# Layer 0's scan output and z gate kept as features by tokens: two heads on the two halves of the array, both directions' states in one product, the RMS norm applied to the projection's result

## The chip, the cores and the metric

The kernel runs on one core of one Trainium2 chip. The metric is the device time of one execution, in microseconds (us). Lower is better. The engines of the core have a queue each and work through it in order: TensorE (PE, with its weight loads PEld), VectorE (DVE), ScalarE (ACT), GpSimd (POOL), and SyncE (SP), which issues the transfers.

## What is computed

Two layers of a diffusion trunk for 1024 latent tokens and 128 context tokens, width 1024, all in float32. Only layer 0's second branch matters here, a bidirectional Mamba-2 scan with 16 heads of 64 features, 2 groups and a state of 64, in chunks of 128 tokens. Cut down:

```python
decay = exp(where(causal, cum[l] - cum[s], -inf))          # per head, direction, chunk of 128 tokens
scores = einsum("bclhn,bcshn->bclsh", C, B) * decay
y_diag = einsum("bclsh,bcshp->bclhp", scores, x * dt)      # inside the chunk
y_off = einsum("bclhn,bchpn,bclh->bclhp", C, h_in, exp(cum))   # from the state that enters the chunk
y = y_fwd + flip(y_bwd) + d_skip[:, None] * x
s_out = rms_norm(y * silu(z), gnorm_w)                     # over the 1024 features of a token
out = concat([a_out, s_out]) @ w_out                       # a_out: the attention branch, 512 features
```

There are nine chunks: eight of latent tokens (numbers 0 to 7) and one of context tokens (number 8, `NLT`), which has no entering state.

## The kernel before

Products with weights are float32 made of two rounded parts (`split` makes a high part on ACT and a low part on DVE), three matmuls each (`mm3`, L256 to L258). Float32 matmuls that are not split appear in the trace as two instructions each.

The program is written as one stream of calls. A scheduler sets each engine's queue from it; `weave` mixes two generators call by call. Tiles are taken by tag with a number of buffers, and whoever takes the tag's next buffer waits for its last reader. The stages, in order of time:

1. Norm, modulation, keys and values of layer 0.
2. `queries` (18 calls) woven with `zproj`. `zproj` makes the gate z in four slabs of 256 columns. For each slab and each of nine token tiles, `tok_proj` runs 24 matmuls with tokens as the stationary operand and 256 moving columns; ACT takes a tanh, DVE finishes the silu (without its factor), and a transfer stores 128 tokens by 256 features in `z_d`.
3. `convs` beside `attention0`: the depthwise convolution makes x, B and C as features by tokens. x is transposed on TensorE and stored as tokens by features in `xs_d`; B and C go to `bc_d`, the states that enter the chunks to `H_d`.
4. `gates0` (attention's gate) woven with `first_outputs`, which runs `scan_out` for the context chunk and for latent chunk 0.
5. The loop that the change is about most: for each chunk c from 1 to 7 `scan_out(c)` stands beside `project_out` of the chunk before it. After the loop follow the last `project_out` and layer 1's latents.
6. Layer 1, which the change does not touch.

`scan_out(c)` loads the chunk's B and C (`BC`), x (`xs`), z (`zs`) and the entering states of both directions (`Hc`: 64 rows for each direction). `Gp` is the product of C and B for the two groups. A "head group" below is four heads, four to a chunk. For each, `cu` (two buffers) is loaded with the cumulated decays of both directions, broadcast to all partitions (L1000). POOL masks each direction (L1003), ACT takes eight exponentials (L1005), DVE adds the two directions (L1007) and multiplies by `G` (L1008), and four matmuls with these 128x128 scores as the stationary operand and 64 columns of x give `yacc` (L1011). The entering states come in through `off`: for each half of the heads and each direction one matmul with 64 rows and 512 columns (L992), scaled by exp(cum) on DVE (L994) and added to y on POOL (L995). At the end DVE adds `yacc` and multiplies by z (L1012, L1013), ACT squares and sums (L1015), POOL makes the reciprocal root (L391, L392), DVE scales y (L1017), TensorE transposes it (L1022) and `split` writes `sT`.

`project_out` accumulates 12 blocks of 128 features (4 of attention, 8 of the scan) in one bank for each half of the columns, and `residual` multiplies by the gate on DVE (L1060) and adds on POOL (L1061). Then come the norm for layer 1 (L1094, L1096) and `norm_T` (L1049, L1052, L1053), which transposes and stores to `h1_d`.

Of the kernel before, what the change touches and what calls it, by code (L numbers as in the profile page):

```python
# [220 lines left out]
def hybrid_trunk(ctx: ExitStack, tc: tile.TileContext, I, O, dbg=None, stage=99):  # L221
# [60 lines left out]
    z_d = scratch("z_d", [T, D])  # L282
# [105 lines left out]
    def rstd_of(p, ssq, n, width):  # L388

        r = p.tile([128, width], F32, tag="rstd", name="rstd", bufs=4)  # L390
        pool.tensor_scalar(r, ssq, 1.0 / n, EPS, ALU.mult, ALU.add)  # L391
        pool.tensor_tensor(r, r, minus_half, ALU.pow)  # L392
        return r
# [81 lines left out]

    lp = Space(mem, right=True)
    nb = lp.tile([128, 2, W16], F32, name="nb", at="F")
    ex = lp.tile([128, 2, W16], F32, name="ex", at="F")
    dskip = lp.tile([128, 16], F32, name="dskip", at="F")
    wdt = lp.tile([128, 2, W16], F32, name="wdt", at="F")  # L480
    decL = lp.tile([128, NLT, 16], F32, name="decL", at="F")
    dma.dma_start(dskip, bcast_rows(I["ab_d_skip"][0], 128))

    def coefficients(p):
# [34 lines left out]
        for d in range(2):  # L519
# [4 lines left out]
            act.activation(ex[:, d], pt[:, 0:W16], AF.Exp)  # L524
# [17 lines left out]
    with Space(mem) as p:  # L542
# [159 lines left out]

    def fm_proj(w, b, hT, c):

        acc = psum("mm", "acc")
        ws = slice(b * 128, (b + 1) * 128)
        for k in range(KT):
            mm3(acc[:, 0:CH], w[0][:, k, ws], w[1][:, k, ws], hT[c][0][:, k], hT[c][1][:, k], k == 0, k == KT - 1)
        return acc[:, 0:CH]
# [137 lines left out]
    def convs(p):  # L847
# [18 lines left out]
        for n, sb in enumerate(order):  # L866
            for b in range(2):
# [19 lines left out]
                if fb < 9:  # L887
# [74 lines left out]
    heads = lambda v: v.rearrange("p (h d) -> p h d", d=64)  # L962
    sTs = {}

    def scan_out(p, sp, c):
        tok = slice(c * 128, (c + 1) * 128)
# [11 lines left out]
        zs = p.tile([128, D], F32, tag="zs", name="zs", bufs=2)  # L978
        dma.dma_start(zs, z_d[tok])
# [4 lines left out]
        y = p.tile([128, D], F32, tag="y", name="y", bufs=2)  # L984
        pool.tensor_tensor(heads(y), heads(xs), dskip.unsqueeze(2).broadcast_to([128, 16, 64]), ALU.mult)
        for g in range(2):
            cs = slice(g * 512, (g + 1) * 512)
            if c < NLT:
                for d in range(2):
                    off = psum("pre", "off")  # L990
                    ds = slice(d * 64, (d + 1) * 64)
                    pe.matmul(off, BC[ds, 1, g], H[ds, cs], start=True, stop=True)  # L992
                    t = p.tile([128, 512], F32, tag="rt", name="off", bufs=2)
                    dve.tensor_tensor(heads(t), heads(off), ex[:, d, c * 16 + g * 8:c * 16 + g * 8 + 8].unsqueeze(2).broadcast_to([128, 8, 64]), ALU.mult)  # L994
                    pool.tensor_tensor(y[:, cs], y[:, cs], t, ALU.add)  # L995
            acc = psum("o" if c < NLT else "pre", "yacc")
            for u in range(2):
                h0 = c * 16 + g * 8 + u * 4
                cu = p.tile([128, 4, 2, 128], F32, tag="cu", name="cu", bufs=2)
                dma.dma_start(cu, bcast_rows(cum_d[h0:h0 + 4], 128))  # L1000
                for d in range(2):
                    s = 1 - 2 * d
                    pool.affine_select(cu[:, :, d], cu[:, :, d], [[0, 4], [s, 128]], ALU.is_ge, NEG, base=0, channel_multiplier=-s)  # L1003
                    for j in range(4):
                        act.activation(cu[:, j, d], cu[:, j, d], AF.Exp, bias=nb[:, d, h0 + j:h0 + j + 1])  # L1005
                m = cu[:, :, 0]
                dve.tensor_tensor(m, m, cu[:, :, 1], ALU.add)  # L1007
                dve.tensor_tensor(m, m, G[:, g].unsqueeze(1).broadcast_to([128, 4, 128]), ALU.mult)  # L1008
                for j in range(4):
                    hc = (u * 4 + j) * 64  # L1010
                    pe.matmul(acc[:, hc:hc + 64], m[:, j], xs[:, g * 512 + hc:g * 512 + hc + 64], start=(u == 0 and j == 0), stop=(u == 1 and j == 3))  # L1011
            dve.tensor_tensor(y[:, cs], acc, y[:, cs], ALU.add)  # L1012
            dve.tensor_tensor(y[:, cs], y[:, cs], zs[:, cs], ALU.mult)  # L1013
        ssq = p.tile([128, 1], F32, tag="ssq", name="ssq", bufs=4)
        act.activation(zs, y, AF.Square, accum_out=ssq)  # L1015
# [680 lines left out]
```

## Time and profile before

| | before |
|---|---|
| median of three runs | 1849.1 us (1843.53 to 1849.83) |
| the profiled execution | 1849.66 us, its span from first to last instruction 1847.8 us |
| mean granted TensorE clock | 0.958 |
| TensorE busy | 1713.8 us, 93% of the span |
| VectorE, ScalarE, GpSimd busy | 1045.4 us, 817.2 us, 744.2 us |
| the stage of queries and z | about 90 to 300 us of the span |
| convolutions and layer 0's attention | about 300 to 630 us |
| attention's gates and the first two scans | about 630 to 768 us |
| five even rounds of the loop of scan and projection | about 768 to 922 us |

Matmuls are pipelined and their ends are modelled, so a busy TensorE is not a full one: what a matmul costs is read from one start to the next. The rows of a stage tell more than the page's shares, since the stages have different limits.

### The profile page before, as it was taken

The page shows a single profiled execution, that of the slowest core. Times are in us where ns is not written, and L with a number is a line of the kernel's source. Part 1 is how long each engine was busy: PE and PEld are TensorE (multiplying, and loading weights), DVE is VectorE, ACT ScalarE, POOL GpSimd, SP SyncE. Part 2 cuts the span into 40 slices and gives each one's busy share as a digit, 9 for nine tenths or more (in the row PEclk, how much of TensorE's full clock was granted, in tenths as well). Part 3 has the DMA queues.
Part 4 walks back from the last instruction along what each step waited for, and adds up shares of the span by engine and source line. Part 5 has one row for each costly group of instructions (what it writes and reads, how often), then busy time and mean ns, then how long its engine had stood idle before and what let it go on. Part 6 is the DMA issues. An engine that isn't in the chain of part 4 may idle for free.

```text
span 1847.8 us, 27078 instructions
## 1 busy us (share of the span) xinstructions
PE 1713.8 (93%) x9031; PEld 1315.1 (71%) x9031; DVE 1045.4 (57%) x1989; ACT 817.2 (44%) x1873; POOL 744.2 (40%) x741
## 2 busy tenths in 40 slices
PE   6899999999998878998899999999999998998898
PEld 3799999877775766666688898655665665654486
DVE  4665545655546467777665434655665664564243
ACT  4532323665655354444444322444545544545321
POOL 3510000133343345665623010466666665565432
PEclk9999999999999888999999999899999998999899
DMA  7423423434435697565463532020120121104342
GB/s 260 125 81 93 121 62 111 131 101 132 115 105 146 195 284 240 166 208 159 167 180 85 165 110 79 11 61 23 52 71 23 45 75 28 37 29 122 109 154 91
DMA packets 210655, 210.26 MB, mean 114 GB/s; under 512 B 36162, under 2 KB 175504, under 8 KB 210516
## 3 DMA queue, kind: packets, MB, share of 16 engines
q1 hardware_dynamic: 210372, 208.40, 37.8%
q8 instruction: 72, 1.18, 0.3%
q14 instruction: 67, 0.55, 0.1%
q0 software_dynamic: 144, 0.13, 0.0%
HBM read 151.94 MB, written 51.72 MB: 110 GB/s over the span
## 4 chain that ended last, share of the span: by engine, by line
PE 65%; DMA 11%; DVE 8%; POOL 4%; ACT 3%; issue 3%; SPq 2%; POOLq 0%; DVEq 0%; ACTq 0%
PE acc L256 12%; PE acc L258 12%; PE acc L257 12%; PE acco L1469 6%; PE sc L1448 3%; PE pp L1427 3%; PE sc L1450 3%; PE sc L1449 3%; DMA arenaG<-cum_d 2%; DVE arenaR L250 2%; DMA arenaF<-rd_d 2%; DMA rd_d<-arenaF 2%; PE st L808 1%; DVE arenaF L209 1%; POOL arenaG L1003 1%
## 5 line engine op out<-in xcount | busy, mean ns | idle before, releaser
L256 PE MATMUL acc<-arenaR 128*128 128x384 f32 (+4 forms) x1248 | 426.7, 343 | 20.0 <-ACT arenaR L249 8.0
L1484 POOL TENSOR_TENSOR arenaG<-arenaG 128x512 f32<-128x512 f32 x256 | 332.6, 1318 | 233.8 <-ACT arenaG L1455 201.1
L257 PE MATMUL acc<-arenaR 128*128 128x384 f32 (+3 forms) x1176 | 398.2, 339 | 0.1
L258 PE MATMUL acc<-arenaR 128*128 128x384 f32 (+4 forms) x1152 | 385.9, 336 | 0.2
L256 PEld LDWEIGHTS acc<-arenaR 128*128 128x128 f32 x1248 | 240.0, 193 | 61.7 <-issue 16.0
L1455 ACT ACTIVATE arenaG<-sc 128x512 f32<-128x512 f32 (+1 forms) x304 | 174.7, 580 | 224.2 <-PE sc L1450 206.7
L209 DVE TENSOR_REDUCE arenaF<-pp 128x1 f32<-128x384 f32 (+1 forms) x400 | 198.8, 539 | 102.2 <-PE pp L1427 100.2
L257 PEld LDWEIGHTS acc<-arenaR 128*128 128x128 f32 x1176 | 226.4, 193 | 15.7 <-issue 3.6
L258 PEld LDWEIGHTS acc<-arenaR 128*128 128x128 f32 x1152 | 221.6, 192 | 16.5 <-DVE arenaR L250 2.3
L250 DVE TENSOR_TENSOR arenaR<-arenaF,arenaR 128x512 fp32r<-128x512 f32 (+2 forms) x144 | 133.2, 938 | 73.3 <-ACT arenaR L249 68.5
L249 ACT CAST arenaR<-arenaF 128x512 fp32r<-128x512 f32 (+3 forms) x160 | 101.0, 649 | 138.9 <-issue 22.6
L1469 PE MATMUL acco<-arenaG 128*64 128x512 f32 (+1 forms) x608 | 152.0, 612 | 0.0
L1005 ACT ACTIVATE arenaG<-arenaG,arenaF 128x128 f32<-128x128 f32 x288 | 88.4, 389 | 113.0 <-POOL arenaG L1003 112.7
L1427 PE MATMUL pp<-arenaR 96*128 96x384 f32 (+1 forms) x300 | 97.6, 387 | 12.8 <-DVE arenaF L209 12.5
L749 POOL TENSOR_TENSOR arenaG<-arenaF,arenaG 128x512 fp32r<-128x512 f32 x28 | 47.8, 1708 | 150.8 <-PE acco L753 87.0
L1448 PE MATMUL sc<-arenaR 96*128 96x512 f32 (+1 forms) x228 | 94.9, 416 | 5.6 <-ACT arenaG L1455 5.4
L1427 PEld LDWEIGHTS pp<-arenaR 96*128 96x128 f32 x300 | 58.6, 203 | 57.3 <-DVE arenaF L209 28.4
L1450 PE MATMUL sc<-arenaR 97*128 97x512 f32 (+1 forms) x228 | 90.6, 400 | 1.0 <-DMA arenaR<-arenaF 1.0
L258 PE MATMUL acc<-arenaR,arenaS 128*128 128x512 f32 (+1 forms) x240 | 90.6, 382 | 0.0
L1449 PE MATMUL sc<-arenaR 96*128 96x512 f32 (+1 forms) x228 | 89.9, 394 | 0.0
L1469 PEld LDWEIGHTS acco<-arenaG 128*64 128x64 f32 x608 | 37.3, 141 | 71.4 <-issue 68.3
L1003 POOL TENSOR_SCALAR_AFFINE_SELECT arenaG<-arenaG 128x512 f32<-128x512 f32 x72 | 60.2, 859 | 63.3 <-DMA arenaG<-cum_d 56.4
(328 smaller groups left out, 3331.9 us busy)
## 6 DMA issues: line engine op xcount, KB each, us to landing
arenaF<-in_ada_w_dram SPq DMA_DIRECT2D x96, 256.0 KB
arenaG<-cum_d SPq DMA_DIRECT2D x36, 512.0 KB
arenaF<-in_ab_w_in_dram SPq DMA_DIRECT2D x51, 256.0 KB
z_d<-arenaF SPq DMA_DIRECT2D x36, 128.0 KB
xs_d<-arenaF SPq DMA_DIRECT2D x8, 576.0 KB
arenaF<-xs_d SPq DMA_DIRECT2D x9, 512.0 KB
arenaF<-z_d SPq DMA_DIRECT2D x9, 512.0 KB
x_d<-arenaG SPq DMA_DIRECT2D x9, 512.0 KB
```

The source lines that it names most:

```text
L209: f()
L250: lo_eng.tensor_tensor(lo, src, hi.bitcast(F32), ALU.subtract)
L256: pe.matmul(out, ah, bh, start=first, stop=False)
L257: pe.matmul(out, ah, bl, start=False, stop=False)
L258: pe.matmul(out, al, bh, start=False, stop=last)
L1427: pe.matmul(pp[:, 0:w], AQ[s][0:96, t * 128:(t + 1) * 128], AK[s][0:96, k0:k0 + w], start=True, stop=True)
L1448: pe.matmul(sc[:, 0:n], AK[s][0:96, ks], BQ[s][:, qs], start=True, stop=False)
L1449: pe.matmul(sc[:, 0:n], BK[s][:, ks], AQ[s][0:96, qs], start=False, stop=False)
L1450: pe.matmul(sc[:, 0:n], AK[s][:, ks], AQ[s][:, qs], start=False, stop=True)
L1455: act.activation(pf, sc[:, 0:n], AF.Exp, scale=SCALE_M)
L1469: put = lambda: pe.matmul(acc[0][a * 64:(a + 1) * 64], V[:, a], pfs[a], start=(i < 2 and k < 2), stop=(last and k >= len(todo) - 2))
L1484: pool.tensor_tensor(totals[a], first[a] if i == 1 else totals[a], pfs[a], ALU.add)
```

## The change

- `zproj` uses `fm_proj`: the slab's weights are the stationary operand and 384 tokens move, so z comes out as features by tokens. 24 calls take the place of 36, and `z_d` is eight blocks of 128 features by all tokens.
- `convs` stores x as features by tokens too (`xT_d`), and `scan_out` loads it into `y` and multiplies it by `d_skip` there.
- `yacc` is now features by tokens: 64 features of a head are the stationary operand (64 columns) and the 128x128 scores move. Heads alternate between partitions 0 to 63 and 64 to 127 of the accumulator, that is between the halves of the array's columns.
- The states come in by the same accumulation: `Cx` is exp(cum) of both directions (two ACT instructions of 64 partitions, L1008) times C (one DVE instruction, L1009); its 128 rows are the two directions' 64 states, so one matmul for each head takes in both. L992, L994, L995 and the table `ex` are gone.
- y is not scaled and not transposed. `split` takes it as it is. Its squares are summed over feature blocks on DVE (L1031) and over partitions by a matmul with ones (L1033); ACT copies the sum (L1035).
- `project_out` accumulates attention's part and the scan's part in two banks; ACT copies the first (L1105), DVE multiplies the second by the token's norm factor and adds (L1106), POOL multiplies by the gate (L1107) and adds (L1108).

```diff
         def zproj(zp, w):
             for q in range(4):
-                for t in range(NT):
-                    acc = tok_proj(t, w, 256)
-                    th = zp.tile([128, 256], F32, tag="zth", name="zth", bufs=3)
-                    act.activation(th, acc, AF.Tanh)
-                    dve.scalar_tensor_tensor(th, th, 1.0, acc, ALU.add, ALU.mult)
-                    dma.dma_start(z_d[t * 128:(t + 1) * 128, q * 256:(q + 1) * 256], th)
-                    if t == 6 and q < 3:
-                        wn = zw(q + 1)
-                    yield
+                for b in range(2):
+                    for c in range(NCH):
+                        acc = fm_proj(w, b, hT, c)
+                        th = zp.tile([128, CH], F32, tag="zth", name="zth", bufs=3)
+                        act.activation(th, acc, AF.Tanh)
+                        dve.scalar_tensor_tensor(th, th, 1.0, acc, ALU.add, ALU.mult)
+                        dma.dma_start(z_d[q * 2 + b, :, c * CH:(c + 1) * CH], th)
+                        if b and c == 1 and q < 3:
+                            wn = zw(q + 1)
+                        yield
...
-            weave(queries(qp, wq), 18, zproj(qp, wz), 36)
+            weave(queries(qp, wq), 18, zproj(qp, wz), 24)
...
                     if fb < 8:
+                        dma.dma_start(xT_d[fb][:, 0:NL], th[:, 0:NL])
+                        dma.dma_start(xT_d[fb][:, NL:T], th[:, NL + 2:W])
...
-        for g in range(2):
-            cs = slice(g * 512, (g + 1) * 512)
+        for u in range(4):
+            g, h0 = u // 2, c * 16 + u * 4
+            if u % 2 == 0:
+                acc = psum("o" if c < NLT else "pre", "yacc")
+            cu = p.tile([128, 4, 2, 128], F32, tag="cu", name="cu", bufs=2)
+            dma.dma_start(cu, bcast_rows(cum_d[h0:h0 + 4], 128))
             if c < NLT:
+                Cx = p.tile([128, 4, 128], F32, tag="Cx", name="Cx", bufs=2)
                 for d in range(2):
-                    off = psum("pre", "off")
-                    ds = slice(d * 64, (d + 1) * 64)
-                    pe.matmul(off, BC[ds, 1, g], H[ds, cs], start=True, stop=True)
-                    t = p.tile([128, 512], F32, tag="rt", name="off", bufs=2)
-                    dve.tensor_tensor(heads(t), heads(off), ex[:, d, c * 16 + g * 8:c * 16 + g * 8 + 8].unsqueeze(2).broadcast_to([128, 8, 64]), ALU.mult)
-                    pool.tensor_tensor(y[:, cs], y[:, cs], t, ALU.add)
+                    r = slice(d * 64, (d + 1) * 64)
+                    act.activation(Cx[r], cu[r, :, d], AF.Exp)
+                dve.tensor_tensor(Cx, Cx, BC[:, 1, g].unsqueeze(1).broadcast_to([128, 4, 128]), ALU.mult)
...
+            todo = [(xs, m, j) for j in range(4)] + ([(H, Cx, j) for j in range(4)] if c < NLT else [])
+            for n, (left, right, j) in enumerate(todo):
+                a, b = j % 2, u % 2 * 2 + j // 2
+                in_order(n, acc[a * 64:(a + 1) * 64, b * 128:(b + 1) * 128], left[:, (u * 4 + j) * 64:(u * 4 + j + 1) * 64], right[:, j],
+                         start=(u % 2 == 0 and n < 2), stop=(u % 2 == 1 and n >= len(todo) - 2))
...
-        dve.tensor_scalar(y, y, r, None, ALU.mult)
-        sT = sp.tile([128, 2, KT, 128], F32R, tag="sT", name="sT", bufs=2)
-        for q in range(2):
-            pt = psum("tr", "pt")
-            for j in range(4):
-                pe.transpose(pt[:, j * 128:(j + 1) * 128], y[:, (q * 4 + j) * 128:(q * 4 + j + 1) * 128], ident)
-            split(sT[:, 0, q * 4:q * 4 + 4], sT[:, 1, q * 4:q * 4 + 4], pt.rearrange("p (k n) -> p k n", k=4))
+        sT = sp.tile([128, 2, KT, 128], F32R, tag="sT", name="sT", bufs=2)
+        split(sT[:, 0], sT[:, 1], y)
+        act.activation(zs, y, AF.Square)
+        sq = p.tile([128, 128], F32, tag="sq", name="sq", bufs=1, at="G")
+        dve.tensor_reduce(sq, zs.rearrange("p k n -> p n k"), AX.X, ALU.add)
+        pt = psum("tr", "pt")
+        pe.matmul(pt[:, 0:1], sq, one, start=True, stop=True)
...
-            acc = psum("mm", "acc")
-            for k in range(12):
-                h, l = (at[:, 0, k], at[:, 1, k]) if k < 4 else (sT[:, 0, k - 4], sT[:, 1, k - 4])
-                mm3(acc, h, l, *wos[k, q], k == 0, k == 11)
-            residual(p, q, acc, x, gate)
+            plain, scaled = psum("pre", "acca"), psum("mm", "accs")
+            for k in range(4):
+                mm3(plain, at[:, 0, k], at[:, 1, k], *wos[k, q], k == 0, k == 3)
+            for k in range(8):
+                mm3(scaled, sT[:, 0, k], sT[:, 1, k], *wos[k + 4, q], k == 0, k == 7)
+            tmp = p.tile([128, 512], F32, tag="rt", name="rt", bufs=2)
+            act.copy(tmp, plain)
+            dve.scalar_tensor_tensor(tmp, scaled, r, tmp, ALU.mult, ALU.add)
+            pool.tensor_tensor(tmp, tmp, gate[:, cs], ALU.mult)
+            pool.tensor_tensor(x[:, cs], x[:, cs], tmp, ALU.add)
```

How the queues stand in the loop, at three places. In these rows a float32 matmul is one row entry, not two. First TensorE at the end of a scan. Before (L256 to L258 are `project_out`'s products, L1049 layer 1's transposes):

```order
L992 MATMUL off<-arenaG,arenaF 128x512
L973 MATMUL Gp<-arenaF 128x128 x2
L1011 MATMUL yacc<-arenaF,arenaG 128x64 x4
L1022 MATMUL pt<-ident,arenaF 128x128 x8
L992 MATMUL off<-arenaG,arenaF 128x512 x2
L256 MATMUL acc<-arenaR,arenaS 128x512
```

TensorE with the change, at a head group between the products of a projection:

```order
L256 MATMUL accs<-arenaR,arenaS 128x512
L257 MATMUL accs<-arenaR,arenaS 128x512
L258 MATMUL accs<-arenaR,arenaS 128x512
L984 MATMUL Gp<-arenaF 128x128 x2
L971 MATMUL yacc<-arenaG,arenaF 64x128 x4
L971 MATMUL yacc<-arenaG 64x128 x4
```

The transposes of y and the four products of the states are gone, and each head group has eight matmuls of 128 moving columns (L971 is the helper `in_order`); in some rounds two groups stand one behind the other.

VectorE at the end of a scan, before (L1096 and L250 into arenaR belong to `project_out`):

```order
L1017 TENSOR_SCALAR arenaF<-arenaF 128x1024
L994 TENSOR_TENSOR arenaG<-off,arenaF 128x512
L1007 TENSOR_TENSOR arenaG<-arenaG 128x4x128
L1096 TENSOR_SCALAR arenaG<-arenaG,arenaF 128x1024
L250 TENSOR_TENSOR arenaR<-arenaG,arenaR 128x512
L1008 TENSOR_TENSOR arenaG<-arenaG,arenaF 128x4x128
```

VectorE behind the end of a scan with the change (L1016 and L1017 are now the two steps of the scores, L1116 the former L1096):

```order
L250 TENSOR_TENSOR arenaS<-arenaF,arenaS 128x1024
L1031 TENSOR_REDUCE arenaG<-arenaG 128x128
L1116 TENSOR_SCALAR arenaG<-arenaG,arenaF 128x1024
L1009 TENSOR_TENSOR arenaG<-arenaG,arenaF 128x512
L250 TENSOR_TENSOR arenaR<-arenaG,arenaR 128x512
L1016 TENSOR_TENSOR arenaG<-arenaG 128x4x128
L1017 TENSOR_TENSOR arenaG<-arenaG,arenaF 128x4x128
```

The two steps of the scores stand together here, and the norm's steps stand ahead of the next group's scores instead of between its two steps.

ScalarE over one round before, beginning with three head groups' exponentials:

```order
L1005 ACTIVATE arenaG<-arenaG,arenaF 128x128 x24
L1015 ACTIVATE arenaF<-arenaF 128x1024
L1094 ACTIVATE arenaG,arenaF<-arenaG 128x1024
L1005 ACTIVATE arenaG<-arenaG,arenaF 128x128 x8
L249 CAST arenaR<-arenaG 128x512
L975 COPY arenaF<-Gp 128x256
L249 CAST arenaS<-pt 128x512 x2
```

ScalarE with the change, from the end of one scan into the next:

```order
L1014 ACTIVATE arenaG<-arenaG,arenaF 128x128 x8
L1114 ACTIVATE arenaG,arenaF<-arenaG 128x1024
L249 CAST arenaS<-arenaF 128x1024
L1029 ACTIVATE arenaG<-arenaF 128x1024
L1008 ACTIVATE arenaG<-arenaG 64x512 x2
L1008 ACTIVATE arenaF<-arenaG 64x512 x2
L1014 ACTIVATE arenaG<-arenaG,arenaF 128x128 x16
L1035 COPY arenaF<-pt 128x1
L1105 COPY arenaF<-acca 128x512
```

Two exponentials for `Cx` (L1008) now stand ahead of each head group's eight (L1014), and L1012, POOL's mask, can overwrite a direction of `cu` only behind the exponential that reads it.

More of the change, by code (lines that the diff above doesn't have):

```diff
@@ L388, in rstd_of @@
     def rstd_of(p, ssq, n, width):
[L390 removed]
+        r = p.tile([128, width], F32, tag="rstd", name="rstd", bufs=5)
         pool.tensor_scalar(r, ssq, 1.0 / n, EPS, ALU.mult, ALU.add)
@@ L474, in tok_proj, with fm_proj @@
         return acc[:, 0:n]
+    def fm_proj(w, b, hT, c):
+        acc = psum("mm", "acc")
+        ws = slice(b * 128, (b + 1) * 128)
+        for k in range(KT):
+            mm3(acc[:, 0:CH], w[0][:, k, ws], w[1][:, k, ws], hT[c][0][:, k], hT[c][1][:, k], k == 0, k == KT - 1)
+        return acc[:, 0:CH]
     lp = Space(mem, right=True)
     nb = lp.tile([128, 2, W16], F32, name="nb", at="F")
-    ex = lp.tile([128, 2, W16], F32, name="ex", at="F")
-    dskip = lp.tile([128, 16], F32, name="dskip", at="F")
+    dskip = lp.tile([128, KT], F32, name="dskip", at="F")
+    one = lp.tile([128, 1], F32, name="one", at="F")
+    pool.memset(one, 1.0)
     wdt = lp.tile([128, 2, W16], F32, name="wdt", at="F")
     decL = lp.tile([128, NLT, 16], F32, name="decL", at="F")
-    dma.dma_start(dskip, bcast_rows(I["ab_d_skip"][0], 128))
+    for a in range(2):
+        dma.dma_start(dskip[a * 64:(a + 1) * 64], bcast_rows(I["ab_d_skip"][0].rearrange("(b a) -> a b", a=2)[a], 64))
     def coefficients(p):
@@ L700, in hybrid_trunk @@
         return
-    def fm_proj(w, b, hT, c):
-        acc = psum("mm", "acc")
[L706 to L709, printed above, removed]
     def silu_of(sp, acc):
@@ L960, in gates0, with in_order @@
             yield
-    heads = lambda v: v.rearrange("p (h d) -> p h d", d=64)
-    sTs = {}
+    sTs, rs = {}, {}
+    def in_order(n, *a, **k):
+        m = pe.matmul(*a, **k)
+        if n:
+            tc.keep_in_program_order(m)
     def scan_out(p, sp, c):
@@ L995, in scan_out @@
[L995 to L1003, printed above, removed]
-                    for j in range(4):
[L1005 to L1008, printed above, removed]
-                for j in range(4):
-                    hc = (u * 4 + j) * 64
-                    pe.matmul(acc[:, hc:hc + 64], m[:, j], xs[:, g * 512 + hc:g * 512 + hc + 64], start=(u == 0 and j == 0), stop=(u == 1 and j == 3))
@@ new lines, in scan_out @@
+                    act.activation(Cx[r], cu[r, :, d], AF.Exp)
+                dve.tensor_tensor(Cx, Cx, BC[:, 1, g].unsqueeze(1).broadcast_to([128, 4, 128]), ALU.mult)
+            for d in range(2):
+                s = 1 - 2 * d
+                pool.affine_select(cu[:, :, d], cu[:, :, d], [[0, 4], [s, 128]], ALU.is_ge, NEG, base=0, channel_multiplier=-s)
+                for j in range(4):
+                    act.activation(cu[:, j, d], cu[:, j, d], AF.Exp, bias=nb[:, d, h0 + j:h0 + j + 1])
@@ L1039, in hybrid_trunk @@
     if stage <= 4:
-        dbg("S", a_d, H_d, cum_d, ex, nb)
+        dbg("S", a_d, H_d, cum_d, nb)
         return
@@ L1049, in norm_T @@
                 pe.transpose(pt[:, j * 128:(j + 1) * 128], xh[:, (q * 4 + j) * 128:(q * 4 + j + 1) * 128], ident)
-            full = p.tile([128, 4, 128], F32, tag="nf", name="nf", bufs=1)
+            full = p.tile([128, 4, 128], F32, tag="rt", name="nf", bufs=2)
             bc = lambda v: v[:, l, q * 4:q * 4 + 4, cond].unsqueeze(2).broadcast_to([128, 4, 128])
```

32 lines of the change are left out of this document (19 added, 13 removed).

## The prediction

> **What bounds the kernel now.** I read the page first, then the stages' busy times, then the chain of work and the waits of the loop, then TensorE's starts in order of time. The page:
>
> ```profile
> PE 1713.8 (93%) x9031; PEld 1315.1 (71%) x9031; DVE 1045.4 (57%) x1989; ACT 817.2 (44%) x1873; POOL 744.2 (40%) x741
> ```
>
> TensorE is the busiest by far, so the question for each stage is whether it is full there. Busy time of the engines in three stages (columns: from and to, length, busy PE, PEld, DVE, ACT, POOL with instructions, granted clock, DMA share, GB/s):
>
> ```profile
> 90.00:300.00 210.00, 208.83 (x1691) 206.52 (x1690) 116.36 (x365) 62.98 (x181) 16.47 (x27) 1.00 0.32 96
> 630.00:768.00 138.00, 120.31 (x553) 96.15 (x553) 92.31 (x129) 63.84 (x163) 68.90 (x68) 0.86 0.76 234
> 768.00:922.00 154.00, 136.41 (x654) 103.79 (x652) 111.57 (x135) 67.22 (x198) 95.81 (x96) 0.94 0.54 174
> ```
>
> In the stage of queries and z TensorE never stops (208.8 of 210). In the first two scans (630 to 768) it is idle 18 us, with the DMA engines at 0.76. The loop (768 to 922) is five rounds. Its chain of work, over one round and a bit:
>
> ```profile
> 772.46 1.10 PE yacc L1011 x8
> ...
> 804.13 1.10 PE yacc L1011 x8
> ...
> 813.68 0.85 PE yacc L1011 x8
> ...
> 814.65 3.66 DMA arenaG<-cum_d
> ...
> 824.72 1.23 POOL arenaG L995
> ...
> 829.11 1.68 DVE arenaG L1096
> 830.78 2.31 DVE arenaR L250
> ...
> 834.18 1.10 PE yacc L1011 x8
> ```
>
> The same place comes back at 772.46, 804.13 and 834.18: a round is (834.18 - 772.46) / 2 = 30.9 us. From 804.13 to 814.5 the chain is TensorE's; then a head group frees its `cu` buffer, the next load takes 3.66, and mask, exponentials, the states' sum on POOL and the norm's steps on VectorE follow until TensorE gets its scores at 834.18. So a round hangs on both TensorE's order and the way of one head group. Who waits there (us in total over five rounds, times, longest):
>
> ```profile
> ACT arenaG L1005 <- POOL arenaG L1003: 76.1, 16, 8.7
> PE yacc L1011 <- DVE arenaG L1008: 11.6, 5, 2.9
> DVE arenaG L1017 <- POOL arenaF L392: 8.8, 3, 2.9
> ...
> PE pt L1022 <- DVE arenaG L1017: 3.8, 3, 1.3
> PE pt L1022 <- DVE arenaF L1017: 2.2, 2, 1.2
> ```
>
> TensorE waits once a round for scores (11.6 / 5 = 2.3 us) and once for the scaled y (6.0 / 5 = 1.2), because VectorE stands 2.9 us before L1017 until POOL has the norm's factor.
>
> **The change part by part.** *z.* The starts of z's matmuls now, 256 columns (first two rows, three apart), and of 384 columns as `fm_proj` runs them in another stage (last two, nine apart):
>
> ```profile
> 270.78 0.28 PE L256 MATMUL acc<-arenaS,arenaR 128*128 128x256 f32 x1
> 271.14 0.28 PE L256 MATMUL acc<-arenaS,arenaR 128*128 128x256 f32 x1
> ...
> 1099.79 0.33 PE L258 MATMUL acc<-arenaR 128*128 128x384 f32 x1
> 1101.35 0.33 PE L258 MATMUL acc<-arenaR 128*128 128x384 f32 x1
> ```
>
> That is 0.12 and 0.173 us each. Before, 36 x 24 = 864 at 0.12 = 103.7; with the change 24 x 24 = 576 at 0.173 = 99.7. TensorE is full there, so 4 us less, of which I take 3.6, since the clock and the mix vary. The cover that shrinks is the next slab's: it is asked for two z calls ahead of its use now (2 x 24 x 0.12 = 5.8 us, with a query between), then one (4.2 us). If its arrival fell short by the difference at all three slabs, 4.8 us would be lost; queries' matmuls stand between and hide it, so I take nothing. ACT and VectorE have fewer and larger pieces and stay far from full.
>
> *TensorE in the loop.* One round's pieces (starts, so that modelled ends don't count):
>
> ```profile
> 816.95 1.00 PE L1011 MATMUL yacc<-arenaF,arenaG 128*128 128x64 f32 x8
> 817.88 1.12 PE L992 MATMUL off<-arenaG,arenaF 64*128 64x512 f32 x2
> 818.93 0.50 PE L256 MATMUL acc<-arenaR 128*128 128x512 f32 x1
> ...
> 827.96 1.58 PE L1022 MATMUL pt<-ident,arenaF 128*128 128x128 f32 x8 [1.22 <-DVE arenaF L1017]
> 829.47 2.08 PE L992 MATMUL off<-arenaG,arenaF 64*128 64x512 f32 x4
> 831.48 0.65 PE L256 MATMUL acc<-arenaR,arenaS 128*128 128x512 f32 x1
> ...
> 1235.23 0.40 PE L1449 MATMUL sc<-arenaS,arenaR 96*128 96x512 f32 x1
> 1235.56 0.44 PE L1469 MATMUL acco<-arenaG 128*64 128x128 f32 x4
> 1235.93 0.27 PE L1412 MATMUL pt<-ident,arenaF 128*4 128x128 f32 x1
> ```
>
> Scores: four groups at 817.88 - 816.95 = 0.93, 3.7 us. States: eight instructions, two at 1.05 twice and four at 2.01, 4.1 us. Transposes of y: 1.51. Together 9.3 us a round. The new form is in the trace already: layer 1's L1469, 64 stationary columns, 128 moving, heads alternating between halves, four instructions in 1235.93 - 1235.56 = 0.37 with the way in and out. A head group has 16: 1.48, four groups 5.9, and the two instructions of L1033 as two of L1011, 0.23: 6.1 us. TensorE saves 3.2 us a round.
>
> The price's ends come from the chain of work, one form that stays on one half and L1469 with 512 columns:
>
> ```profile
> 475.16 1.24 PE st L808 x10
> ...
> 1173.56 1.87 PE acco L1469 x8
> ```
>
> Without any overlap of halves 64 x 0.124 + 0.23 = 8.2 (saves 1.1); with a quarter of the 512-column price, 64 x 1.87 / 8 / 4 + 0.23 = 4.0 (saves 5.3). I take L1469 with 128 columns, the same shape.
>
> Here a rule speaks against the change. Between L1449 and the four L1469 stand 0.33 us, where 0.23 is usual, so going into the halves costs about 0.1. The Trainium skill, TensorEngine Tiling (Array Packing), Key Properties, says that "Changing tiling mode (not just tile) drains the TensorE". Were a drain a whole matmul's 0.40 (the row of L1449) on each way in and out, eight a round, it would take 3.2 us, all of the saving; the trace's 0.37 for four with both ways agrees with a short drain only.
>
> *The other engines in the loop.* Rows of the groups over the five rounds, and below them the nearest rows of the whole trace:
>
> ```profile
> L1008 DVE TENSOR_TENSOR arenaG<-arenaG,arenaF 128x512 f32<-128x512 f32 x20 | 20.4, 1020 | 0.5
> L994 DVE TENSOR_TENSOR arenaG<-off,arenaF 128x512 f32<-128x512 f32 x20 | 13.7, 682 | 6.0 <-POOL arenaG L1061 6.0
> ...
> L250 DVE TENSOR_TENSOR arenaS<-pt,arenaS 128x512 fp32r<-128x512 f32 x10 | 6.4, 675 | 0.0
> ```
> ```profile
> L250 DVE TENSOR_TENSOR arenaR<-arenaF,arenaR 128x1024 fp32r<-128x1024 f32 x15 | 25.4, 1693 | 19.1 <-ACT arenaR L249 19.0
> L824 ACT COPY arenaS<-st 64x512 f32<-64x512 f32 x16 | 9.2, 577 | 10.4 <-PE st L808 10.3
> L209 DVE TENSOR_REDUCE arenaF<-pp 128x1 f32<-128x384 f32 x384 | 195.2, 549 | 101.1 <-PE pp L1427 99.3
> ```
>
> VectorE has 111.6 / 5 = 22.3 us a round. It loses L994 (4 x 0.68 = 2.7), two lows of `sT` (1.35) and L1017 with its wait; it gains L1009 four times (as L1008, 4.1), the low of `sT` in one (1.7) and L1031 (1024 elements against 384: 1.5): about 25 us, still under the round. ScalarE has 13.4 and gains eight `Cx` exponentials at 0.58 (4.6) and two copies (1.2): about 19. POOL has 19.2, loses four L995 (1.2 each) and gains two products by the gate (as L995 too): about 17. The transfers grow by 512 KB a round; a round at 174 GB/s is 5.4 MB, so by a tenth, at a share of 0.54.
>
> *Waits.* The 1.2 us before the transposes goes with them. The wait for scores stays and its way gets longer: two exponentials stand ahead of the masks, 2 x 0.58 = 1.2 us, and VectorE's added work, (25 - 22.3) / 4 = 0.6 for a group. What is late next is that group's L1017. So a round gains 3.2 + 1.2 - 1.2 - 0.6 = 2.6 us. Seven scans (chunks 1 to 7) stand beside projections: 18 us.
>
> *The first two scans.* TensorE has 18 us to spare there, so its saving counts nothing; 1 MB more for x (4.5 us at 234 GB/s if transfers set the end, nothing if they don't) is hidden by the same spare time. I take 0, with -4 to +4.5 as ends. The 4.7 MB of x stored in the convolutions' stage, 16 more issues on SP's queue, lie behind 330 us of TensorE's work: 0.
>
> Sum: 3.6 + 18.2 = 21.8 us off the profiled execution's 1849.66, 1827.9. The median of the runs is 0.6 lower, 1849.1, so I say 1828.
>
> **The rivals.** *The loop doesn't move, only z does.* What TensorE gives up turns into waits, as the chain leaves TensorE for 20 of 31 us already. For it: 76.1 us of waits of ACT behind POOL's masks. Against: TensorE's own order is the chain from 804.13 to 814.5, and two waits a round fall away. 1849.1 - 3.6 = 1845. A drain at 0.40 each way ends here too.
>
> *Slower: head groups that stand in pairs.* The queue with the change has two groups' exponentials behind each other in some rounds. With both `cu` buffers freed together, ScalarE does 2 x (1.2 + 2.45) in a row (2.45 is one group's eight), and TensorE has nothing else ready: the second group comes 1.2 + 1.2 later than now, 2.4 us a round with no TensorE saving seen, 7 x 2.4 - 3.6 = +13: 1862. It decides where load, ScalarE's 7.3 and VectorE's two steps for the second group (as L1008, 1.0 each: 3.7 + 7.3 + 2.0 = 13.0) are longer than what TensorE has to do between two pairs, half a round without waits and savings: (30.9 - 3.5 - 3.2) / 2 = 12.1. That is close, but only some rounds have pairs. The row of the eight:
>
> ```profile
> 819.11 2.45 ACT L1005 ACTIVATE arenaG<-arenaG,arenaF 128x128 f32<-128x128 f32 x8 [6.41 <-POOL arenaG L1003]
> ```
>
> *Much faster.* The norm's factor no longer stops VectorE, its scores come in time, and a round falls to VectorE's 25 us: 7 x 5.9 + 3.6 = 45, 1804. Against: no engine in the loop runs at more than nine tenths now.
>
> **How the numbers follow.** Forecast 0.62 (own range 1815 to 1840: 1.0 to 4.4 us a round, the first scans' ends), only z 0.18, slower 0.12, much faster 0.08. From 1806 to 1850 leaves out most of the slow case and the lower half of the much faster one, under 2 in 10. A measurement tells about 0.5%, 9 us: faster than 1840 has 0.69 (0.62 x 0.98 and 0.08), within 0.19, slower 0.12.
>
> **What would show it.** Right: rounds of about 28 us; L971 groups of 16 in about 1.5 us from start to start; the stage of queries and z about 3.6 us shorter; no engine waiting for L392 at the end of a scan. Wrong: 16 instructions taking 2 us; rounds at 31 with TensorE's waits for L1017 grown by what it saved; TensorE idle before a slab's first matmul in z; transfers of x and z late in the first two scans.

## The result: slower by 1.15%, and the profile after

The changed kernel takes 1871.7 us (median of four runs, 1869.1 to 1881.5) against 1849.5 before; the ratio is 1.0115, with an interval from 1.0088 to 1.0142. I had said 1828, from 1806 to 1850: the sign is wrong, and that the size is nearly the same is chance. The profiled run took 1872.8, with a span of 1871.0 against 1847.8. Of the page, the engines' row:

```profile
PE 1696.0 (91%) x8881; PEld 1302.8 (70%) x8881; DVE 1043.1 (56%) x1968; ACT 865.4 (46%) x1932; POOL 728.0 (39%) x728
```

TensorE is busy 18 us less than before (1713.8), as it should be, and the span is 23 us longer: all that was saved, and as much again, is now waiting. Where it arises is read from fixed points of the program, in us from the start of each profiled run (a "round" is a sixth of the time from the first norm's transposes of layer 1's input to the seventh; "loop" is from the first to the ninth and last):

| profiled run of | first query scored | last (latent tokens) | last product of the chunk states | first norm | round | loop | first heads of layer 1 | span |
|---|---|---|---|---|---|---|---|---|
| before | 131 | 296 | 645 | 744 | 30.4 | 223 | 1141 | 1848 |
| changed | 140 | 318 | 661 | 749 | 32.2 | 251 | 1165 | 1871 |
| e1, skip factors by rows | 132 | 305 | 646 | 743 | 32.5 | 254 | 1163 | 1868 |
| e3, no states | 139 | 317 | 662 | 763 | 28.9 | 226 | 1163 | 1868 |
| e5, third buffer | 140 | 318 | 662 | 757 | 28.7 | 221 | 1147 | 1849 |
| e6, before with a third buffer | 129 | 294 | 646 | 743 | 29.8 | 220 | 1137 | 1841 |
| e9, z late | 143 | 315 | 642 | 734 | 31.8 | 246 | 1147 | 1849 |
| e10, three mends | 134 | 305 | 648 | 743 | 28.4 | 225 | 1135 | 1837 |

So three places lose: the start (9 us), the end of the queries (12 more) and the loop (28). Of the loop's 28 us, 11 arise in the six rounds and 17 behind the seventh norm. Two stretches give time back. One is behind the ninth norm, 8 us: the changed kernel has 72 of layer 1's products (416 columns) ahead of that norm, the one before 48, so a part of the loop's 28 us is work that only moved. The other is between the last query and the first norm, 16 us, a gain that I had put at nothing. Whether it is TensorE's saving in the first scans isn't shown: e5, which differs by the loop's buffers alone, takes 95 us from the last product of the chunk states to the first norm, and the changed kernel 88.

**The start.** Bytes moved over the first 60 us in 40 slices of 1.5 us, before:

```profile
GB/s 0 46 29 85 388 350 345 363 365 306 358 370 391 328 317 322 338 252 247 292 270 274 154 186 192 259 257 320 317 203 81 2 172 84 320 210 168 358 396 371
```

The same for the changed kernel, and the two issues of the skip factors there:

```profile
GB/s 0 46 29 96 377 355 365 363 373 340 294 323 388 229 50 52 58 82 90 182 351 276 248 222 175 309 217 213 199 262 204 294 285 297 220 138 0 150 187 327
```
```profile
14.62 0.76 SPq L493 DMA_DIRECT2D arenaF<-in_ab_d_skip_dram  x1
...
16.77 0.95 SPq L493 DMA_DIRECT2D arenaF<-in_ab_d_skip_dram  x1
```

From the 15th to the 19th slice the rate falls to 50 to 90 GB/s, right behind these two issues. `dskip` is now read with every second element for one half: 128 partitions times 8 pieces of 4 bytes. They carry 4 KB and hold up the first weights for some 8 us. From 14 to 30 us the trace has 1176 packets under 512 bytes, and 285 in e1 below, where these pieces are gone. The Trainium skill, DMA: Bandwidth & Descriptors, Rules for kernel authors, says that a strided last dimension is lowered to one descriptor for each element; the trace agrees.

**The end of the queries.** Busy times in one stretch there, before and after (columns as in the prediction):

```profile
300.00:330.00 30.00, 30.00 (x179) 28.31 (x178) 16.10 (x17) 13.83 (x30) 2.05 (x1) 1.00 0.21 70
```
```profile
300.00:330.00 30.00, 21.46 (x117) 19.14 (x116) 16.05 (x43) 6.42 (x20) 0.00 (x0) 0.85 0.20 59
```

TensorE, full before, stands idle. It waits three times, 2 us each, for a query's maximum, with no other matmul queued ahead of these transposes (changed kernel, 311 to 328 us):

```profile
PE pt L682 <- DVE arenaS L678: 6.1, 3, 2.2
PE sc L743 <- DVE arenaF L663: 1.2, 1, 1.2
```

**The loop.** Busy times over about six rounds, before and after:

```profile
743.00:926.00 183.00, 163.17 (x792) 124.24 (x790) 130.71 (x160) 82.75 (x242) 114.28 (x115) 0.95 0.54 172
```
```profile
748.00:942.00 194.00, 161.27 (x928) 124.10 (x927) 135.77 (x157) 120.07 (x296) 101.74 (x104) 0.90 0.65 193
```

ScalarE went from 82.8 to 120.1 and the DMA share from 0.54 to 0.65. The largest wait of any engine there is ScalarE's, for the loads of `cu` (us in total, times, longest):

```profile
ACT arenaF L1008 <- DMA arenaG<-cum_d: 33.9, 10, 6.7
```

Now two head groups and what they wait for, in order of time: first the issues of their `cu` loads, then the other engines.

```profile
813.84 1.30 SPq L1003 DMA_DIRECT2D arenaG<-cum_d  x2
```
```profile
819.76 1.29 ACT L1008 ACTIVATE arenaF<-arenaG 64x512 f32<-64x512 f32 x2 [6.67 <-DMA arenaG<-cum_d]
...
820.46 1.80 POOL L1012 TENSOR_SCALAR_AFFINE_SELECT arenaG<-arenaG 128x512 f32<-128x512 f32 x2 [1.62 <-ACT arenaF L1008]
...
821.13 1.28 ACT L1014 ACTIVATE arenaG<-arenaG,arenaF 128x128 f32<-128x128 f32 x4
...
822.32 1.26 ACT L1008 ACTIVATE arenaG<-arenaG 64x512 f32<-64x512 f32 x2
...
824.79 0.56 ACT L1105 COPY arenaF<-acca 128x512 f32<-128x512 f32 x1
824.97 0.69 DVE L1016 TENSOR_TENSOR arenaG<-arenaG 128x512 f32<-128x512 f32 x1 [0.67 <-ACT arenaG L1014]
...
825.40 0.71 PE L984 MATMUL Gp<-arenaF 64*128 64x128 f32 x4 [3.27 <-ACT arenaF L1105]
...
825.73 2.45 ACT L1014 ACTIVATE arenaG<-arenaG,arenaF 128x128 f32<-128x128 f32 x8
...
826.24 0.68 DVE L1017 TENSOR_TENSOR arenaG<-arenaG,arenaF 128x512 f32<-128x512 f32 x1
```

The two loads take 6 us, ScalarE does both groups' work in one row, and the copy of the plain sum (L1105) stands between the groups' exponentials, so that TensorE waits 3.27 us for the bank that the copy frees.

**The end of the loop.** From the seventh norm to the ninth, before and after:

```profile
925.60:966.80 41.20, 40.56 (x207) 34.87 (x206) 27.31 (x38) 17.47 (x39) 11.29 (x18) 1.00 0.63 187
```
```profile
942.10:999.90 57.80, 45.83 (x235) 38.14 (x236) 32.12 (x41) 24.22 (x53) 21.32 (x27) 0.88 0.51 147
```

TensorE is idle 12.0 us there, where it was idle 0.6. The last scan now ends when nothing else stands ahead of its projection in TensorE's queue, and the longest wait is for ScalarE's `split` of the whole y:

```profile
967.58 0.80 PE L256 MATMUL accs<-arenaR,arenaS 128*128 128x512 f32 x1 [4.95 <-ACT arenaS L249]
```

No run edits this place alone.

### The profile page after: what moved, and what is told of

Read it like the earlier page. It is cut to its first block, busy times and chain, and to the rows that moved or that the text cites. A ratio compares the mean times of both kernels' runs of the same rounds, so it can differ in the third digit from the quotient of the medians.

```text
span 1871.0 us, 26764 instructions
## 1 busy us (share of the span) xinstructions
PE 1696.0 (91%) x8881; PEld 1302.8 (70%) x8881; DVE 1043.1 (56%) x1968; ACT 865.4 (46%) x1932; POOL 728.0 (39%) x728
## 3 DMA queue, kind: packets, MB, share of 16 engines
q8 instruction: 70, 1.15, 0.3%
## 4 chain that ended last, share of the span: by engine, by line
PE 38%; DMA 9%; DVE 5%; ACT 4%; issue 2%; SPq 1%; POOL 1%; DVEq 0%; POOLq 0%; ACTq 0%
PE acco L1489 6%; PE acc L256 5%; PE acc L257 5%; PE acc L258 5%; PE sc L1468 3%; PE pp L1447 3%; PE sc L1470 3%; PE sc L1469 3%; DMA arenaG<-cum_d 2%; DMA arenaF<-rd_d 2%; DMA rd_d<-arenaF 1%; PE den L1520 1%; ACT arenaG L1014 1%; DVE arenaR L250 1%; DVE arenaF L209 1%
## 5 line engine op out<-in xcount | busy, mean ns | idle before, releaser
L256 PE MATMUL acc<-arenaR 128*128 128x384 f32 (+4 forms) x1128 | 391.5, 348 | 32.4 <-ACT arenaR L249 11.2
L257 PE MATMUL acc<-arenaR 128*128 128x384 f32 (+3 forms) x1056 | 362.2, 343 | 0.1
L258 PE MATMUL acc<-arenaR 128*128 128x384 f32 (+4 forms) x1032 | 351.1, 341 | 0.1
L256 PEld LDWEIGHTS acc<-arenaR 128*128 128x128 f32 x1128 | 218.0, 194 | 67.4 <-ACT arenaR L249 12.9
L257 PEld LDWEIGHTS acc<-arenaR 128*128 128x128 f32 x1056 | 203.8, 193 | 12.5 <-issue 2.8
L258 PEld LDWEIGHTS acc<-arenaR 128*128 128x128 f32 x1032 | 199.8, 194 | 12.8 <-DVE arenaR L250 1.6
L250 DVE TENSOR_TENSOR arenaR<-arenaF,arenaR 128x512 fp32r<-128x512 f32 (+2 forms) x144 | 126.8, 892 | 91.9 <-ACT arenaR L249 89.0
L752 POOL TENSOR_TENSOR arenaG<-arenaS,arenaG 128x512 fp32r<-128x512 f32 x26 | 43.6, 1678 | 157.5 <-PE acco L756 84.0
L1447 PEld LDWEIGHTS pp<-arenaR 96*128 96x128 f32 x300 | 59.3, 206 | 56.7 <-DVE arenaF L209 28.7
L1014 ACT ACTIVATE arenaG<-arenaG,arenaF 128x128 f32<-128x128 f32 x288 | 88.8, 389 | 14.1 <-POOL arenaG L1012 13.1
L1012 POOL TENSOR_SCALAR_AFFINE_SELECT arenaG<-arenaG 128x512 f32<-128x512 f32 x72 | 60.9, 855 | 83.2 <-ACT arenaF L1008 47.8
L250 DVE TENSOR_TENSOR arenaR<-acc,arenaR 64x512 fp32r<-64x512 f32 (+2 forms) x84 | 48.3, 579 | 62.6 <-ACT arenaR L249 61.2
```

Of the source, the lines that this page charges most:

```text
L250: lo_eng.tensor_tensor(lo, src, hi.bitcast(F32), ALU.subtract)
L256: pe.matmul(out, ah, bh, start=first, stop=False)
L257: pe.matmul(out, ah, bl, start=False, stop=False)
L258: pe.matmul(out, al, bh, start=False, stop=last)
L1447: pe.matmul(pp[:, 0:w], AQ[s][0:96, t * 128:(t + 1) * 128], AK[s][0:96, k0:k0 + w], start=True, stop=True)
```

## The experiments

Each time is a median, each ratio that of its runs to the runs of the kernel before beside it.

**e1: the skip factors by rows**

```diff
-        dma.dma_start(dskip[a * 64:(a + 1) * 64], bcast_rows(I["ab_d_skip"][0].rearrange("(b a) -> a b", a=2)[a], 64))
+    dma.dma_start(dsk, bcast_rows(I["ab_d_skip"][0], 128))
...
+        pool.tensor_copy(dskip[e], dsk[e].rearrange("p (b a) -> p b a", a=2)[:, :, a])
```

> The changed kernel with the skip factors loaded as one row of 16 to every partition and sorted into the halves' order on the chip, instead of element by element. Theory of the start: the 1024 pieces of 4 bytes hold the queue for some 9 us in which the first weights should come (53 to 90 GB/s there against 320 to 390); the first query starts at 131 instead of 140 us and the whole is about 8 us shorter, 1863 to 1865. Rival, taken back later: the convolutions and the first scans gave back 8 of the 13 us by which they began late, so the start's 9 are hidden by a limit that comes later, and the whole stays at 1869 to 1873.

Measured: 1865.8, ratio 1.0085 (1.0051 to 1.0118). In its first 60 us the trough is gone:

```profile
GB/s 0 47 29 110 374 333 341 363 371 326 385 408 404 378 382 382 326 214 266 257 291 201 195 184 286 266 277 353 198 47 10 112 194 320 162 164 333 372 355 298
```

The first query is scored at 132 us, 8 earlier, and the last product of the chunk states comes 15 earlier; then a longer stretch to the first norm and a longer loop take most of it. The times of this run and of the changed kernel differ by 6 us, within their intervals; e7 against e5 shows the step more clearly.

**e2: z alone, in the kernel before**

```diff
-                for t in range(NT):
-                    acc = tok_proj(t, w, 256)
+                for b in range(2):
+                    for c in range(NCH):
+                        acc = fm_proj(w, b, hT, c)
```

> The kernel before with z alone changed (features by tokens, 24 calls of 384 columns); the scan reads z in rows of 4 KB of the new layout, so y is multiplied by other elements of z. My prediction's reason: 3.6 us less, 1845. Theory of the queries' way: the stage is set by the way of 18 queries, not by TensorE's columns; shorter z calls only draw the convolutions' calls ahead of the queries, whose last two then stand without cover: the last query's end 8 to 12 us later than before, of which the convolutions take back a part, the whole 1852 to 1860.

Measured: 1860.2, ratio 1.0050 (1.0021 to 1.0078): slower by 8 us, where my prediction's term says 4 faster. The four transposes of a query start every 10.2 us before (138.2 for the second, 290.5 for the seventeenth) and every 11.1 here; the last query is scored 14 us later.

**e3: without the states, and e4: one sum**

```diff
-            if c < NLT:
-                Cx = p.tile([128, 4, 128], F32, tag="Cx", name="Cx", bufs=2)
...
-            todo = [(xs, m, j) for j in range(4)] + ([(H, Cx, j) for j in range(4)] if c < NLT else [])
+            todo = [(xs, m, j) for j in range(4)]
```

> The changed kernel without the states' part of y: no exponentials and products into Cx, eight instructions instead of sixteen into the halves. Theory of the head groups: a round is two times the way of a group in a ring of two, which these exponentials made longer by 1.3 us at the least; without them the way is 9.7 to 10.5 us again, a round 3 to 4 us shorter and the whole 1845 to 1853. Rival, the norm's end: rounds are set by the sum in two parts and by what its copies wait for; then only ScalarE's time beside it goes, and the whole is 1862 to 1870.

Measured: 1869.6, ratio 1.0116 (1.0072 to 1.0161). Both theories missed a part. The rounds fell by 3.3 us to 28.9, as the head groups' theory says, and the loop by 25. But the stretch from the last product of the chunk states to the first norm grew from 88 to 102 us: the transfers' share (a packet's time counts where it starts, so the share can pass 1) is 1.04 to 1.08 there from 681 to 741 us, where it is 1.03, 0.83 and 0.71 in the changed kernel's three stretches of 20 us from 680. The whole moved by 2 us. Why that stretch grew isn't shown; e5, which has the changed kernel's code there, takes 95.

```diff
-            plain, scaled = psum("pre", "acca"), psum("mm", "accs")
...
+            acc = psum("mm", "acc")
...
+            residual(p, q, acc, x, gate)
```

> The changed kernel with the projection summed in one accumulator as before and the norm's factor left out of the result (it is still worked out). Theory of the head groups: ScalarE's two copies and two products on POOL go, TensorE no longer waits for the copy (8.7 us over eight rounds), the whole 1862 to 1866. Rival, the norm's end: the copies that stand behind a store and behind the other sum are what stops ScalarE and so the scores; without them rounds fall to 29 us and below, and the whole is 1845 to 1855.

Measured: 1876.6, ratio 1.0152 (1.0100 to 1.0205), rounds 32.9. Both theories expected a gain and there is none in the whole or in the rounds. The loop, at 247, is 4 us shorter, so the two sums and their copies aren't what it loses most by.

**e5: a third `cu` buffer, e6: the same in the kernel before, e7: with the skip factors by rows**

```diff
         gate = load_gate(p, 0, 1)
+        p.widen("cu", at="G")
...
-        x = p.tile([128, D], F32, tag="x", name="x", bufs=2)
+        x = p.tile([128, D], F32, tag="x", name="x", bufs=1)
```

> The changed kernel with a third cu buffer in the loop (its room is taken from the second buffer of x, whose load has a whole round). Theory of the head groups: a round is twice the way from TensorE's end with a group to the scores of the group that takes its buffer (12.3 us in the changed kernel, 5 to 6 of it the load); with the load done ahead the way falls to 7 or 8, rounds from 32 to 27 to 29 us, and the whole to 1848 to 1856. Rival, transfers and ScalarE's order: the load only moves ahead and waits stay behind the masks, the split of y and the copies; rounds stay at 31 to 33, the whole at 1866 to 1873.

> The kernel before with the same third cu buffer (x with one). Theory of the head groups: its ring too set the round (one way of 16.2 us in each, 9.7 of it before VectorE's stop); TensorE's wait of 2.3 us a round for scores goes, seven rounds, 1836 to 1842. Rival: its rounds hang on TensorE's own order and the stop of VectorE for the norm's factor, which stays; 1847 to 1853.

> The changed kernel with both: the skip factors loaded by rows, and the third cu buffer. If the start's time and the head groups' add up, 6 us below the run with the buffer alone, 1842 to 1850. If what begins earlier only waits later (transfers between the gates and the first scans are busy nine tenths of the time), within 2 us of the run with the buffer alone.

Measured: e5 1854.8, ratio 1.0026 (0.9996 to 1.0055); e6 1841.1, 0.9932 (0.9906 to 0.9958); e7 1841.1, 0.9929 (0.9904 to 0.9955). One more buffer is worth 17 us in the changed kernel and 11 in the one before. In the changed kernel the rounds fall from 32.2 to 28.7, so there the ring set the round. In the kernel before they fall only from 30.4 to 29.8, and its loop from 223 to 220: another limit stood as near as the ring, and the profile doesn't show where the rest of the 11 us comes from. With the start mended too (e7 against e5), the median falls by another 14, where it fell by 6 in e1; the profiled runs of e5 and e7, 1850.8 and 1846.6, differ by 4 only. So the start's loss reaches the end better once the ring no longer sets the loop, but how much of it is not well known. The loop's stretch in e5, DMA share 0.70 against 0.65:

```profile
757.00:929.00 172.00, 151.43 (x915) 115.02 (x915) 140.97 (x158) 120.90 (x304) 101.92 (x103) 0.93 0.70 208
```

**e8: x and z in rows of 4 KB**

```diff
-        dma.dma_start(y, xT_d[:, :, tok].rearrange("k p n -> p k n"))
+        dma.dma_start(y.rearrange("p k n -> p (k n)"), xT_d.rearrange("k p t -> (k p t)").rearrange("(t d) -> t d", d=D)[tok])
```

> The changed kernel with x and z of a scan read in rows of 4 KB instead of pieces of 512 bytes (the same bytes, other elements of them in y). Theory of the pieces: 16600 pieces more in the loop's stretch take 31 us of all 16 engines there and delay the cu loads that stand behind them (5 to 6 us against 3.7); rows fall to 30 us, the whole to 1855 to 1862. Theory of the head groups alone: the loads are a little shorter only, 1866 to 1872.

Measured: 1866.6, ratio 1.0085 (1.0059 to 1.0112), rounds 31.5: the head groups' case. By the medians the pieces of 512 bytes cost 5 us, which the intervals don't tell from nothing.

**e9: z handed out late, and e13: the same in the kernel of e2**

```diff
-            weave(queries(qp, wq), 18, zproj(qp, wz), 24)
+            weave(queries(qp, wq), 18, zproj(qp, wz), 14)
```

> The changed kernel with z's 24 calls handed out more slowly beside the queries (14 over the 18 queries, the rest behind), nothing else. Theory of the queries' way: the queries set the stage, z's calls were used up too early and the convolutions' calls drawn ahead of the queries, so that the last two stand bare; with calls of z left for them the convolutions' first block begins before the last query as it did before, and the whole falls by 6 to 9 us, 1862 to 1866. Rival: a query needs 11.1 us of its own beside calls of 384 columns, so the end of the queries stays where it is and the whole at 1869 to 1873.

> The kernel before with z alone changed, its 24 calls handed out at 14 over the 18 queries; y takes other elements of z, as in the run of z alone (1860.2). My prediction's term, with the order mended: 3.6 us below before, 1846. Theory of the queries' way: the time of that stage is the queries', so TensorE's 4 us don't appear, 1849 to 1852; were the way longer for calls of 384 columns in any order, 1854 to 1860.

Measured: e9 1857.6, ratio 1.0040 (1.0018 to 1.0062), 14 us less than the changed kernel, more than expected. The last query is hardly earlier, at 315 us, but the last product of the chunk states is, by 19, and TensorE is full again at the end of the queries:

```profile
300.00:330.00 30.00, 30.00 (x184) 29.50 (x183) 13.67 (x33) 7.69 (x23) 0.00 (x0) 1.00 0.22 65
```

e13 took 1853.0, ratio 0.9999 (0.9978 to 1.0020): with its order mended, z by features costs nothing, and the 4 us that TensorE saves don't show, though the interval just reaches them.

**e10: three mends, e11: four, e14: another four.** e10 is e7 with z's calls at 12 over the 18 queries. e11 adds blocks for x and z (`xT_d` and `z_d` as `[NT, 128, KT, 128]`). e14 adds to e10 the edit of e12.

> The changed kernel with three mends: skip factors by rows, the third cu buffer, z's calls handed out at 12 over the 18 queries. The two first gave 1841.1. If the queries' end is worth its 8 us here too: 1832 to 1836, ahead of every kernel so far. If the convolutions take up what the queries leave: 1839 to 1843.

> As the run with three mends, and x and z are kept in blocks of one scan's 128 tokens, so that the stores go in pieces of 512 bytes and the scan's loads in rows of 4 KB. Theory of the pieces: the loads that stand in front of the cu loads are shorter (5 us in the changed kernel); 3 to 5 us below three mends. Rival: with the cu loads a buffer ahead nothing waits for a load any more; the same within 2 us, or slower where the stores of z and x now take longer beside the convolutions' own.

> The changed kernel with skip factors by rows, the third cu buffer, z handed out at 12 over the 18 queries, and the hidden state in the place of x. Three mends gave 1838.9. If ScalarE's stand for the stores (10.6 us in that run) delays scores: 1831 to 1836. Rival: the one buffer of x now waits for the stores in its turn and the ends of the rounds stay; 1837 to 1842.

Measured: e10 1838.9, ratio 0.9936 (0.9912 to 0.9960), faster than the kernel before and the lowest median of all; e11 1841.1, 0.9953 (0.9933 to 0.9973); e14 1847.4, 0.9971 (0.9950 to 0.9991). e10 and e11 came out near what their rivals said; e14, 8 us slower than e10, is outside both of its ranges. e10, e7 and e6 can't be told apart. So the mended change is 33 us faster than the change, but no faster than the old kernel with a third buffer.

**e12: a place of its own for the next layer's hidden state.** The change moved `nf` from a buffer of its own into the ring `rt`, where L1105 writes too. What ScalarE stood for ahead of L1105 in the changed kernel:

```profile
  DMA h_d<-arenaF: 14.4, 4
  DMA h_d<-arenaG: 4.8, 3
```

```diff
-            full = p.tile([128, 4, 128], F32, tag="rt", name="nf", bufs=2)
+            full = into[:, q * 512:(q + 1) * 512].rearrange("p (k n) -> p k n", k=4)
...
-        norm_T(p, 1, 0 if t < NLT else 1, xn, tok)
+        norm_T(p, 1, 0 if t < NLT else 1, xn, tok, x)
```

> The changed kernel, only that the next layer's hidden state goes to the place of x (which is done with by then) instead of the ring rt that it shares with the residual's sums. Theory of the shared ring: ScalarE stands 19.2 us before L1105 for the stores of h, and its exponentials and the freeing of the sum's bank stand behind it; without it rounds fall by 1 to 2 us, the whole 1858 to 1865. Rival, the head groups: the ring of two cu buffers still sets the round, and ScalarE's stand only moves to its next wait; 1868 to 1873.

Measured: 1884.3, ratio 1.0163 (1.0132 to 1.0194), rounds 34.1: slower than either theory said. (The profiled run, 1873.4, is the fastest of the six.) The same 19 us stand ahead of the same copy, for another:

```profile
  POOL arenaG L1108: 18.8, 4
```

The stand moved to the next holder of the ring, and the buffers of `x`, now held until the stores of h are done, came late: SyncE stands 8.7 us before four loads of `x` for these stores. The experiment can't tell what the shared ring costs; that stays open.

## Why the prediction was wrong

**The failed step: what TensorE saves in the loop was put on the path.** I subtracted 3.2 us a round for TensorE and then corrected for waits. But in the changed kernel the ring of two `cu` buffers sets the round: a third buffer, which saves TensorE nothing, takes 3.5 us off it (e5). With two buffers, a round of four head groups is twice the circle of one buffer: from TensorE's end with a group, over load, masks, exponentials and scores, to TensorE's end with the group that takes its buffer. The old states' products and the transposes of y are not in this circle. Means over 20 groups (five rounds) of the profiled runs, in us:

| part of the circle | before | changed | e3, no states |
|---|---|---|---|
| buffer free to load issued | 0.17 | 0.28 | 0.60 |
| issue to the first that reads it | 4.42 | 5.18 | 5.08 |
| `Cx` exponentials ahead of the first mask | - | 0.96 | - |
| first mask to last exponential | 3.35 | 3.91 | 3.50 |
| last exponential to scores (VectorE) | 4.18 | 2.20 | 2.57 |
| scores to TensorE | 2.33 | 2.15 | 2.10 |
| TensorE's own | 1.05 | 1.37 | 0.69 |
| twice the sum | 31.0 | 32.1 | 29.1 |
| measured round of these groups | 31.0 | 32.6 | 29.2 |

The parts follow one another without a gap, so twice their sum gives the round in any kernel with two buffers. The sum is no proof that the ring sets the round (that is e5); it tells where a group's time goes. In the kernel before, a third buffer only makes other parts longer: over the same 20 groups of e6, VectorE's part is 7.2 and the wait for TensorE 4.0, and the round stays at 31.0. From before to changed, VectorE's part fell by 2.0 a group, 4 a round (I had taken 1.2 for the stop by the norm's factor), and load, `Cx`, masks and TensorE's own grew by 0.8, 1.0, 0.6 and 0.3. That is 1.1 us a round more, 1.6 as measured, where I had 2.6 less. I had charged the exponentials for `Cx` once a round, 1.2 us; in the circle they count twice, 1.9. My "slower" rival, 1862, named the place (ScalarE with two groups in series) and came nearest.

**TensorE's price in the loop** was right in kind and too high: sixteen instructions took 1.02 us from start to the next matmul (at 831.60), against my 1.48:

```profile
830.58 0.66 PE L971 MATMUL yacc<-arenaG,arenaF 128*64 128x128 f32 x8
831.07 0.61 PE L971 MATMUL yacc<-arenaF,arenaG 128*64 128x128 f32 x8
```

No drain of a whole matmul shows. The saving was larger than I said, on an engine that wasn't the bound of the rounds, and none of it is seen there.

**z.** I read "TensorE never stops" as "TensorE bounds the stage". As e9 and e13 show, it was full because the scheduler fills the time between the steps of a query, with z's matmuls first and then the convolutions'. The step "queries' matmuls stand between and hide it" looked only at the slab's cover; the price was TensorE's idle time at the end of the stage: -3.6 forecast, +8 measured (e2), 0 with the order mended (e13).

**What I never priced.** The skip factors' load stands in the diff, and I gave it no term: about 8 us at the start. Nor did I price the end of the loop, where the last scan stands uncovered: the last product of `project_out` ends at 982.5 us, 24.7 later than before, of which the first norm has 5.1 and the six rounds 11.3, so 8 arise there. The move of `nf` into the ring `rt` stands in the diff too. The x stores in the convolutions' stage, which I put at 0, weren't tried apart; from the last query to the last product of the chunk states it is 343 us with them and 349 before.

**The signs I had named** told the case: rounds at 32 with grown waits, and in z TensorE idle at the stage's end rather than before a slab.

Not settled: alone the three mends take off 6, 14 and 17 us, and 33 together, but z's part, 14 alone, is 2 on top of the other two. The loop of e10 is no shorter than the one before, 225 against 223: its six rounds take 12 us less, and the way from the seventh norm to the ninth 14 more, 54.8 against 41.2, with TensorE idle for 10.4. In most of that loop VectorE has 159 of 200 us, more than any engine but TensorE:

```profile
743.00:943.00 200.00, 175.76 (x1053) 134.97 (x1052) 159.25 (x180) 128.75 (x317) 110.64 (x111) 0.96 0.70 206
```

## To carry over

Where a loop's loads go through a ring, write down the circle of one buffer and price an edit on that circle; an engine that is busy nine tenths of the time may still not be in it. Since the parts of a circle always add up to the round, try one more buffer to see whether the ring binds. Price the loop's last round by itself: what is covered in the middle stands bare there. A full engine beside a slow chain may be full of what the scheduler could find, so a shorter filler can leave it idle at the end of the stage. Read every load in a diff for the length of its contiguous pieces, the small ones most of all.

## What the runs showed of the hardware

A wait of TensorE costs more than its length. After a wait for scores in the changed kernel:

```profile
841.99 1.12 PE L971 MATMUL yacc<-arenaG,arenaF 128*64 128x128 f32 x8 [6.30 <-DVE arenaG L1017]
...
844.48 0.63 PE L257 MATMUL accs<-arenaR,arenaS 128*128 128x512 f32 x1
844.91 0.63 PE L256 MATMUL accs<-arenaR,arenaS 128*128 128x512 f32 x1
...
847.19 0.40 PE L256 MATMUL accs<-arenaR,arenaS 128*128 128x512 f32 x1
847.43 0.39 PE L257 MATMUL accs<-arenaR,arenaS 128*128 128x512 f32 x1
```

The matmuls of 512 columns start every 0.43 us for some 3 us, then every 0.23; the granted clock is 0.50 from 843.0 to 846.6 us and 1.00 from 847 to 850. From 600 to 1060 us slow starts cost some 20 us in the changed kernel and 10 before (each start beyond 0.235 counted, those at a change of form too), which is part of the waits' price here. In the loop, waits of 2.6 us and more were nearly always followed by such a stretch: 2.61 us of waiting at 793.0 by 14 slow matmuls. Shorter waits were at times: before, 1.27 us at 797.9, with a granted clock of 0.50 from 798 to 801. The Trainium skill, TensorE: Matmul & The Clock Gate, Part 1, says that the array falls to half its clock after an idle window of about 3.4 us; the half rate agrees, the trace shows it after shorter waits too.
